# A hybrid decoder step on one core: issuing handed-over operations one step later, loading inner FFN tiles one by one, and pinning three groups of instructions

## The chip, the core and the metric

The kernel runs on one core of a Trainium2 chip. The core has a matrix engine (TensorE, PE in the profile, with a row of its own, PEld, for weight loads), a vector engine (VectorE, DVE), a scalar engine (ScalarE, ACT), a general engine (GpSimd, POOL) and an engine that here only issues transfers (SyncE, SP). Each engine takes its instructions from a queue of its own, in the order in which they stand there; 16 DMA engines move data between main memory and the on-chip memory. The metric is the device time of one execution in microseconds (us); less is better.

## The reference

One layer of a decoder trunk for 1024 prompt tokens and 64 sample tokens (8 sequences of 8 tokens), model width 1024, all in float32:

```python
x = x + 0.5 * swiglu(rmsnorm(x, norm_ffn1), ffn1_w_in, ffn1_w_out)     # inner width 2816
mix, new_pool, new_conv, new_ssm = token_mixing(rmsnorm(x, norm_mix), ...)
x = x + mix
x = x + 0.5 * swiglu(rmsnorm(x, norm_ffn2), ffn2_w_in, ffn2_w_out)
y = rmsnorm(x, norm_final)
```

`token_mixing` projects its input with `w_in`, and merges two branches with sigmoid gates. The pooling branch takes trailing-window means minus the token, multiplies them with a 256x256 matrix per group, scales them and applies `pool_w_out`. The SSD branch runs a causal convolution and a chunked state-space scan (32 heads of 64 in 4 groups, state 128, chunks of 128 tokens), gates its output with silu(z), normalises it in four groups and applies `ssd_w_out`. The merged branches go through `w_o`. The new pooling, convolution and state tensors are outputs as well.

## The kernel before

**Tokens and numbers.** The 1088 token columns are cut into two halves, h = 0 (512 prompt tokens) and h = 1 (512 prompt and 64 sample tokens). Activations lie with channels on the partitions. Every large product is made of three float32r matmuls: weights and activations are each split into a high part (ACT, a copy or identity) and a low part (DVE, source minus high part), and `products` issues high x high, high x low and low x high. `split` (L345 to L351) is that pair for activations, `load_w` (L277 to L296) loads a 256 KB block of weights and splits it. 90 blocks of later weights are split early by the generator `part_weights` (L298 to L311) while the first FFN runs, written to DRAM as two tiles and later read back ready-made (L287).

**Stages.** (1) Load and normalise x (`load_x`); first FFN, input side (`ffn_in_plain`, then `ffn_in`, a seven-product scheme) writing 22 inner tiles per half to DRAM (`hdram`); output side in `ffn`. (2) Input projection: `u_pair`, `z_pair`, `conv_pair`, `gate_pair`, with results written to DRAM. (3) The mix: pooling branch of half 0 and half 1 (`mix_pool`), then `ssd_out(0, 0)`, `mix_out(0)` (which calls `ssd_out(0, 1)` and applies `w_o`), `ssd_out(1, 0)`, `mix_out(1)`. Beside them runs the scan, a background job. (4) The second FFN and the final norm.

**What sets the order.** Background jobs are Python generators ("chains"). The code keeps a clock `pe[0]` that adds up the nominal time of each matmul that it issues; a chain that yields w is taken up again once the clock has moved on by w (`tick`, called after every few matmuls of the main work). The numbers at the head of the file (`STEP`, `GP`, `G_WAIT` and so on) are those yields. `until(c)` steps the chains without waiting for the clock until c has ended. The order in which the code issues instructions is a priority, not the final order: the compiler's scheduler may place an instruction ahead of earlier ones of its engine where it counts it as ready sooner. `tc.high_priority` moves an instruction's priority up.

**Buffers.** Most activation tiles come from one pool, `act`, of 58 buffers; FFN tiles also from `fx` (16), raw weights from `wraw` (6), split weights from `wh` and `wl` (3 each). An instruction that needs a buffer still in use waits at the head of its queue.

**The places that the change touches, before it:**

- Start (L802 to L814): x of half 0 is loaded in eight transfers, then four blocks of weights (`raws`), then x of half 1; the squares of x (L682) and the first `load_w` (L294) share ACT.
- `ffn`, L605 to L642: for each half, after the other half's or the input side's last matmul, all 22 inner tiles are loaded (L619, issued by POOL) and each is split at once (L620), then eight output columns m are accumulated over the 22 tiles.
- `pool_parts` (L1080): loads one tile `dd` of pooled inputs (L1084) and splits it at once (L1086). All eight of half 0 are asked for before the last `gate_pair`; of half 1, four while `mix_pool(0)` runs its last four `out(m)`, the rest inside the groups of `mix_pool(1)` (L1168 to L1170).
- The scan: for each half and group, `ssd_group` goes over 4 or 5 chunks with two steps each. `ssd_a` loads the decay rows `ab` (L1245, two buffers), transposes x (`pxT`), multiplies B and C (`pcb`), makes `cbm`, `btok`, `xp`, `xd` (L1255 to L1267), then `ea`, `ab` on ACT (L1272 to L1275) and the product `ab*cbm` on DVE (L1276). `ssd_st` multiplies `btok` and `xd` (`pst`) and updates the state `hst` (POOL L1361, DVE L1363); `ssd_b` makes the chunk's output (`pyo`, `pyd`, L1342 to L1344), and for the sample chunk handles eight state tiles `h0` (L1295 to L1329) with two loads in flight.
- `gating` (L1404): for each of four tiles a POOL product with z (L1412), at once its square on ACT and the running sum on DVE (`squares`, L364), then `rstd`, then the scaling (L1420) and the store to `yd`. Only two of the four z tiles are loaded ahead.
- `y_load` (L1431): loads eight `yd` tiles back (L1439), then splits one per step.
- `mix_out`, `merge(m)` (L1500): product with the gate, sum with the pooling branch on POOL (L1506), and its split at once.

```python
        def group(gi):                                            # mix_pool, L1167
            for k in range(2 * gi + 2, min(KD, 2 * gi + 6)):
                pool_parts(h, k, True)
            dh, dl = zip(pool_parts(h, 2 * gi), pool_parts(h, 2 * gi + 1))
```

Of the kernel before, what the change touches and what calls it, by code (L numbers as in the profile page):

```python
# [8 lines left out]
F32 = mybir.dt.float32  # L9
F32R = mybir.dt.float32r  # L10
# [33 lines left out]
STEP = (3.3, 3.3)  # L44
SSD0 = (2.0, 2.0)
C_PACE = 1.0
M_AT = (0.5, 1.0)
STEP_S = 1.8
GP = (0.7, 1.2)
# [10 lines left out]
N_PRE, N_DD = 3, 8  # L60
Y_PACE = 0.8
G_WAIT = (7.0, 5.0)
# [4 lines left out]
def tile_hybrid_pool_ssd_macaron(  # L67
# [203 lines left out]
    def raw_w(w, k0, nk, c0, ncol=P):  # L271
        raw = sp.tile([P, 4 * P], F32, tag="wraw", bufs=N_RAW, name=nm("wraw"))[:, : nk * ncol]
        dma(raw.rearrange("p (k c) -> p k c", c=ncol),
            w[k0 * P : (k0 + nk) * P, c0 : c0 + ncol].rearrange("(k p) c -> p k c", p=P))
        return raw

    def load_w(w, k0, nk, c0, ncol=P, raw=None):  # L277
# [15 lines left out]
        with tc.high_priority(hp[0]):  # L293
            S.activation(wh, raw, AF.Copy)  # L294
            V.tensor_tensor(wl, raw, wh.bitcast(F32), op=ALU.subtract)  # L295
# [302 lines left out]
    def ffn(wi, wo, prep, after, half=None, sums=None):  # L598
# [9 lines left out]
        for h in HALVES:  # L608
            for ff in range(NFF - N_APART, NFF):
                ffn_in(wi, ff, [(h, X[h])])  # L610
        for h in HALVES:
            N = NTOK[h]
            parts = [], []
            for k in range(NFF):

# [4 lines left out]
                split(t, a[:, :N], t.bitcast(F32R))  # L620
                parts[0].append(a)
                parts[1].append(t.bitcast(F32R))
            xt = []
            for ms in ((0, 1),) + tuple((m,) for m in range(2, KD)):
                po = [banks([(h,)], "pd", "po")[0] for _ in ms]
                for kb in range(0, NFF, 4):
# [150 lines left out]
    raws = [(kb, c0, raw_w(wi1, kb, 4, c0)) for kb in (0, 4) for c0 in (0, FF)]  # L777
# [4 lines left out]
    for kb, c0, raw in raws:  # L782
        ahead[kb, c0] = load_w(wi1, kb, 4, c0, raw=raw)
# [217 lines left out]
    def pool_out_rows(ost):  # L1001
# [5 lines left out]
        dma(new_pool_s[0, :, 0:7, :], state_pool[0, :, 8:HIST, :])  # L1007
# [72 lines left out]
    def pool_parts(h, k, only=False):  # L1080
        if (h, k) not in dparts:
            N = NTOK[h]
            dd = act((P, N), name="dd")
            dma(dd, ddd[k][:, slice(*TOK[h])])  # L1084
            a = act((P, N), F32R, "dh")
            split(dd, a, dd.bitcast(F32R))  # L1086
            dparts[h, k] = a, dd.bitcast(F32R)
        return None if only else dparts.pop((h, k))
# [40 lines left out]
    for k in range(N_DD):  # L1129
        pool_parts(0, k, True)  # L1130
    gate_pair(14, (1,))
    st.close()
# [29 lines left out]
    def mix_pool(h):  # L1162
# [42 lines left out]
    def sample_parts(g, Bf, xs4, dtd3):  # L1205


        out = []
        for i in range(2):
# [3 lines left out]
            S.copy(xr[:, 4, :].rearrange("p (r t) -> p r t", r=3), Bf[:, tok].unsqueeze(1).broadcast_to([P, 3, 32]))  # L1213
            px, pb = psum("ps", "px3"), psum("ps", "pb3")
            for j in range(4):
# [4 lines left out]
                            dtd3[:, i, g * HPG : (g + 1) * HPG].unsqueeze(2).broadcast_to([96, HPG, HD]), op=ALU.mult)  # L1220
            S.activation(X3, xd, AF.Copy)
            V.tensor_tensor(X3[32:64], xd[32:64], X3[32:64].bitcast(F32), op=ALU.subtract)
            B3 = small((96, P), "B3", 1, F32R)
            S.activation(B3, pb[:96, :P], AF.Copy)
# [3 lines left out]
                            bsel3.unsqueeze(2).broadcast_to([96, 4, P]), op=ALU.mult)  # L1228
            out.append((X3, bb))
        return out  # L1230

    def ssd_a(h, g, c, Bf, Cf, xs4, dts):
# [439 lines left out]
```

## Time and profile before

| what | us |
|---|---|
| median of 3 runs | 3068.37 (3059.94 to 3070.72) |
| the profiled execution | 3074.41 |
| its span, first to last instruction | 3072.5 |
| PE busy | 2888.5 (94%) |
| DVE, ACT, POOL busy | 1600.1, 1314.6, 854.2 |
| mean granted PE clock | 0.972 |

The profile page gives busy time by engine, 40 slices of the span, DMA queues, the chain that ended last and the costliest groups of instructions. The trace can be asked for waits (who waited for whom), for the instructions of a stretch in order of time, and for busy time in stretches of one's choice. "L165" is the line of the helper `mm` and "L169" that of `tr`, so matmuls and transposes are told apart by their tile names: `po` is the FFN's output, `pw` its input side and the projection, `pgm` and `pbp` the pooling branch, `pso` and `pwo` the products with `ssd_w_out` and `w_o`, and `pst`, `pyd`, `pyo`, `pxT`, `pcb` the scan.

### The profile page before, as it was taken

What the parts mean: (1) busy time and instruction counts of PE and PEld (TensorE: products, weight loads), DVE (VectorE), ACT (ScalarE), POOL (GpSimd) and SP (SyncE); (2) the same over time, 40 slices, a digit from 0 to 9 for tenths busy, and PEclk for the clock granted to TensorE, in tenths of its full rate; (3) what the DMA queues carried; (4) which work ended last, traced back from release to release, by engine and by line L of the source; (5) the groups of instructions that cost most, each with busy time, mean ns of one, the idle gap of its engine ahead of it and who ended that gap; (6) DMA issues with size and microseconds to landing.
All of it is one profiled execution on the core that took longest, in us unless ns stands there. A gap on an engine that the chain in (4) does not pass through costs nothing. (4 is left out here: it accounts for less than half of the span.)

```text
span 3072.5 us, 54064 instructions
## 1 busy us (share of the span) xinstructions
PE 2888.5 (94%) x20356; PEld 2721.6 (89%) x20356; DVE 1600.1 (52%) x2834; ACT 1314.6 (43%) x2755; POOL 854.2 (28%) x917
## 2 busy tenths in 40 slices
PE   6999999887999999999999799898899999999998
PEld 5999999667989999999987687777899999997898
DVE  5555445535355677666646565645355433344442
ACT  5344445423233346555556555434223333343332
POOL 4333333110043333333312222432114333332100
PEclk9999999998999999999999899997999999999999
DMA  4477667895353323233358687876775222226542
GB/s 125 145 242 235 204 204 230 287 293 171 105 193 113 106 89 123 87 105 106 108 195 281 226 301 254 277 236 217 252 262 174 88 78 82 71 84 206 167 134 73
DMA packets 531223, 532.33 MB, mean 173 GB/s; under 512 B 41530, under 2 KB 371376, under 8 KB 530954
## 3 DMA queue, kind: packets, MB, share of 16 engines
q1 hardware_dynamic: 523906, 504.37, 51.4%
q0 software_dynamic: 7040, 24.52, 2.2%
q8 instruction: 160, 2.62, 0.4%
q14 instruction: 101, 0.83, 0.1%
q10 hardware_dynamic: 16, 0.00, 0.0%
HBM read 377.09 MB, written 151.90 MB: 172 GB/s over the span
## 5 line engine op out<-in xcount | busy, mean ns | idle before, releaser
L165 PE MATMUL pw<-hi,wh 128*128 128x288 f32 (+1 forms) x2176 | 630.6, 290 | 8.4 <-DVE t L549 5.2
L165 PE MATMUL pw<-X,wh 128*128 128x256 f32 (+1 forms) x3264 | 627.9, 291 | 2.9 <-ACT rb L815 1.7
L165 PE MATMUL pw<-hi,wl 128*128 128x288 f32 (+1 forms) x2176 | 628.7, 289 | 0.7 <-DVE wl L445 0.7
L165 PE MATMUL pw<-lo,wh 128*128 128x288 f32 (+1 forms) x2176 | 628.3, 289 | 0.0
L165 PEld LDWEIGHTS pw<-X,wh 128*128 128x128 f32 x3264 | 519.9, 192 | 4.0 <-ACT rb L815 1.9
L165 PE MATMUL pw<-X,wl 128*128 128x256 f32 (+1 forms) x1632 | 473.3, 290 | 0.0
L165 PEld LDWEIGHTS pw<-hi,wh 128*128 128x128 f32 x2176 | 412.8, 190 | 9.6 <-DVE t L549 5.8
L165 PEld LDWEIGHTS pw<-hi,wl 128*128 128x128 f32 x2176 | 412.6, 190 | 0.9 <-DVE wl L445 0.9
L165 PEld LDWEIGHTS pw<-lo,wh 128*128 128x128 f32 x2176 | 412.7, 190 | 0.0
L445 DVE TENSOR_TENSOR wl<-s,wh 128x512 fp32r<-128x512 f32 x284 | 203.9, 720 | 256.1 <-ACT wh L444 251.9
L165 PEld LDWEIGHTS pw<-X,wl 128*128 128x128 f32 x1632 | 313.0, 192 | 0.2 <-DVE wl L445 0.2
L438 POOL TENSOR_TENSOR s<-wraw,wraw 128x512 f32<-128x512 f32 x142 | 195.2, 1375 | 416.8 <-DVE wl L445 295.1
L165 PE MATMUL po<-hh,wh 128*128 128x288 f32 (+1 forms) x1056 | 290.7, 334 | 17.3 <-ACT hh L347 12.9
L165 PE MATMUL po<-hh,wl 128*128 128x288 f32 (+1 forms) x1056 | 292.7, 332 | 5.1 <-DVE wl L295 4.8
L444 ACT ACTIVATE wh<-s 128x512 fp32r<-128x512 f32 x284 | 179.1, 631 | 269.8 <-PE pw L165 215.2
L165 PE MATMUL po<-hr,wh 128*128 128x288 f32 (+1 forms) x1056 | 293.1, 332 | 0.7 <-DVE hr L349 0.3
L295 DVE TENSOR_TENSOR wl<-wraw,wh 128x512 fp32r<-128x512 f32 x216 | 142.6, 665 | 262.3 <-ACT wh L294 258.2
L294 ACT ACTIVATE wh<-wraw 128x512 fp32r<-128x512 f32 x216 | 127.0, 596 | 305.5 <-PE po L165 249.4
L165 PEld LDWEIGHTS po<-hh,wh 128*128 128x128 f32 x1056 | 181.1, 192 | 36.7 <-ACT hh L347 16.5
L445 DVE TENSOR_TENSOR wl<-wraw,wh 128x512 fp32r<-128x512 f32 x213 | 157.4, 740 | 105.6 <-ACT wh L444 97.6
L444 ACT ACTIVATE wh<-wraw 128x512 fp32r<-128x512 f32 x213 | 134.1, 630 | 182.6 <-PE pw L165 163.3
L165 PEld LDWEIGHTS po<-hh,wl 128*128 128x128 f32 x1056 | 182.7, 192 | 21.9 <-DVE wl L295 7.8
(388 smaller groups left out, 5212.9 us busy)
## 6 DMA issues: line engine op xcount, KB each, us to landing
wraw<-in_ffn_w_in_dram SPq DMA_DIRECT2D x184, 256.0 KB
wraw<-wp SPq DMA_DIRECT2D x180, 256.0 KB
wraw<-in_ffn_w_out_dram SPq DMA_DIRECT2D x160, 256.0 KB
wraw<-in_w_in_dram SPq DMA_DIRECT2D x124, 256.0 KB
wp<-wp SPq DMA_DIRECT2D x90, 256.0 KB
wp<-wr SPq DMA_DIRECT2D x90, 256.0 KB
wh<-wp SPq DMA_DIRECT2D x90, 256.0 KB
wl<-wp SPq DMA_DIRECT2D x90, 256.0 KB
```

The lines of the kernel that those rows point to most:

```text
L165: T.matmul(out, lhsT, rhs, start=start, stop=stop, skip_group_check=free)
L294: S.activation(wh, raw, AF.Copy)
L295: V.tensor_tensor(wl, raw, wh.bitcast(F32), op=ALU.subtract)
L438: G.tensor_tensor(t, a, b, op=op)
L444: S.activation(wh, a, AF.Copy)
L445: V.tensor_tensor(wl, a, wh.bitcast(F32), op=ALU.subtract)
```

## The change

What is computed stays the same; issue order, yields and buffers change.

- **Start.** The four first weight loads and their ACT splits are pinned in program order (`keep_in_program_order` ties an instruction behind the one issued before it on its engine), so they stay behind x of half 0. The copy `new_pool_s <- state_pool` is pinned as well.
- **FFN inner tiles.** Loads become a chain `inner(h)`: one load per 0.4 (half 0) or 0.68 (half 1) of the clock, each split not before 3.5 after its load. Half 0's chain starts 2.0 into the last input column of half 1, half 1's with the last output column of half 0.
- **Pooled inputs.** `pool_parts` becomes `pool_load` and `pool_cut`. Half 0: eight loads, then eight splits at 0.8 each, all beside the last `gate_pair`. Half 1: two loads at each of `out(3)` to `out(6)` of half 0, and their splits one `out` later.
- **Scan.** `ab` is loaded after `ssd_b` of the chunk before; `ea` and `ab` come first in `ssd_a`, `xd` before `xp` and `cbm`; `ab*cbm` becomes `ssd_m`, a step later; the POOL product of the old state moves from `ssd_st` into `ssd_a`; `sample_parts` yields between its parts; three `h0` loads in flight instead of two, their POOL product right after the transposes. Steps: `STEP` 3.3 to 2.9, `SSD0` 2.0 to 3.0, `STEP_S` 1.8 to 1.6, one step fewer per group.
- **Gating.** All four z tiles are loaded ahead; four POOL products, after 6.5 four squares into four tiles, after 2.5 three sums; `G_WAIT` 7.0 to 4.0.
- **y_load and merge.** The DVE half of a split is issued one step after its ACT half; the split of `merge(m)` is issued with `merge(m + 1)`.

```diff
-    raws = [(kb, c0, raw_w(wi1, kb, 4, c0)) for kb in (0, 4) for c0 in (0, FF)]
+    raws = [(kb, c0, raw_w(wi1, kb, 4, c0, pin=True)) for kb in (0, 4) for c0 in (0, FF)]
...
-        ahead[kb, c0] = load_w(wi1, kb, 4, c0, raw=raw)
+        ahead[kb, c0] = load_w(wi1, kb, 4, c0, raw=raw, pin=True)
...
-        dma(new_pool_s[0, :, 0:7, :], state_pool[0, :, 8:HIST, :])
+        tc.keep_in_program_order(dma(new_pool_s[0, :, 0:7, :], state_pool[0, :, 8:HIST, :]))
...
             for k in range(NFF):
                 own = k < 3 if h == 0 else not half and k >= NFF - 2
...
                 G.dma_start(t, hdram[h][k])
-                split(t, a[:, :N], t.bitcast(F32R))
                 parts[0].append(a)
                 parts[1].append(t.bitcast(F32R))
+                todo.append((pe[0], t, a))
+                yield H_PACE[h]
+                while todo and todo[0][0] + H_LAND < pe[0]:
+                    cut()
+            while todo:
+                yield max(0.3, todo[0][0] + H_LAND - pe[0])
+                cut()
...
-            for k in range(2 * gi + 2, min(KD, 2 * gi + 6)):
-                pool_parts(h, k, True)
-            dh, dl = zip(pool_parts(h, 2 * gi), pool_parts(h, 2 * gi + 1))
+            dh, dl = zip(dparts.pop((h, 2 * gi)), dparts.pop((h, 2 * gi + 1)))
...
-            if h == 0 and m >= KD - 4:
-                pool_parts(1, m - KD + 4, True)
+            if h == 0 and m >= KD - 5:
+                for k in range(2 * (m - KD + 5), min(KD, 2 * (m - KD + 5) + 2)):
+                    pool_load(1, k)
+                if m > KD - 5:
+                    for k in range(2 * (m - KD + 4), 2 * (m - KD + 4) + 2):
+                        pool_cut(1, k)
...
         for c in range(n):
-            try:
-                next(ga)
-            except StopIteration as e:
-                a = e.value
-            if c + 1 < n:
-                ga = ssd_a(h, g, c + 1, Bf, Cf, xs4, dts)
-                next(ga)
+            a = yield from ssd_a(h, g, c, ab, Bf, Cf, xs4, dts)
             yield step
             if prev:
-                for w in ssd_b(h, g, *prev, Cf, y4, dts):
-                    yield w
+                yield from ssd_b(h, g, *prev, Cf, y4, dts)
+            if c + 1 < n:
+                ab = ssd_load(h, g, c + 1)
             yield step
+            ssd_m(a)
             prev = (c, a, ssd_st(h, g, c, a, dts))
...
         for j in range(4):
-            if j + 2 < 4:
-                z4.append(act((P, N), name="z"))
-                dma(z4[-1], zd[g * 4 + j + 2][:, slice(*TOK[h])])
             G.tensor_tensor(y4[:, j, :N], z4[j], y4[:, j, :N], op=ALU.mult)
-            squares(sums, y4[:, j, :N])
-            yield GP[0]
+        yield GP[0]
+        sq = [act((P, N), name="sq") for _ in range(4)]
+        for j in range(4):
+            S.activation(sq[j], y4[:, j, :N], AF.Square)
+        yield GP[2]
+        for j in range(1, 4):
+            V.tensor_tensor(sq[0], sq[0], sq[j], op=ALU.add)
```

More of the change, by code (lines that the diff above doesn't have):

```diff
@@ L607, in ffn, with inner, cut @@
             ffn_in(wi, ff, [(h, X[h]) for h in HALVES])
[L608 to L611, printed above, removed]
+        def inner(h):
             N = NTOK[h]
             parts = [], []
+            todo = []
+            def cut():
+                _, t, a = todo.pop(0)
+                split(t, a[:, :N], t.bitcast(F32R))
             for k in range(NFF):
@@ L619, in ffn @@
                 G.dma_start(t, hdram[h][k])
-                split(t, a[:, :N], t.bitcast(F32R))
                 parts[0].append(a)
                 parts[1].append(t.bitcast(F32R))
+                todo.append((pe[0], t, a))
[5 more added lines that the diff above has]
+                cut()
+            return parts
+        hid = {}
+        for h in HALVES:
+            for ff in range(NFF - N_APART, NFF):
+                ffn_in(wi, ff, [(h, X[h])])
+            if h == 0:
+                hid[0] = start(inner(0), H_AT)
+        for h in HALVES:
+            N = NTOK[h]
+            parts = None
             xt = []
@@ L625, in ffn @@
                 po = [banks([(h,)], "pd", "po")[0] for _ in ms]
+                if h == 0 and ms[-1] == KD - 1:
+                    hid[1] = start(inner(1), 1.0)
+                if parts is None:
+                    finish(hid[h])
+                    parts = hid[h].value
                 for kb in range(0, NFF, 4):
@@ L1078, in tile_hybrid_pool_ssd_macaron, with pool_load, pool_cut @@
     dparts = {}
[L1080 to L1088, printed above, removed]
+    def pool_load(h, k):
+        t = act((P, NTOK[h]), name="dd")
+        dma(t, ddd[k][:, slice(*TOK[h])])
+        dparts[h, k] = t
+    def pool_cut(h, k):
+        t = dparts[h, k]
+        a = act((P, NTOK[h]), F32R, "dh")
+        split(t, a, t.bitcast(F32R))
+        dparts[h, k] = a, t.bitcast(F32R)
     xn0 = []
@@ L1128, in tile_hybrid_pool_ssd_macaron, with first_pool @@
     gate_pair(14, (0,))
-    for k in range(N_DD):
-        pool_parts(0, k, True)
+    def first_pool():
+        for k in range(KD):
+            pool_load(0, k)
+            yield 0.3
+        for k in range(KD):
+            yield 0.8
+            pool_cut(0, k)
+    c = start(first_pool(), 0.5)
     gate_pair(14, (1,))
+    finish(c)
     st.close()
@@ L1346, in ssd_st @@
     def ssd_st(h, g, c, a, dts):
-        cd = dts[3]
-        btok, xd = a[4], a[2]
-        hc = c * NH + g * HPG
+        btok, xd, hn_ = a[4], a[2], a[8]
         hold = hstate[g]
@@ L1355, in ssd_st @@
         mm(pst, btok, xd)
-        hn_ = act((P, 512), name="hst")
         with tc.high_priority(HP_ST):
@@ L1442, in y_load @@
         yield 3.0
-        for a, t in zip(*parts):
-            split(t, a, t.bitcast(F32R))
+        for i in range(9):
+            if i < 8:
+                S.activation(parts[0][i], parts[1][i], AF.Copy)
+            if i:
+                a, t = parts[0][i - 1], parts[1][i - 1]
+                V.tensor_tensor(t.bitcast(F32R), t, a.bitcast(F32), op=ALU.subtract)
             yield Y_PACE
```

146 lines of the change are left out of this document (82 added, 64 removed).

## The prediction

> **What bounds the kernel now.** I read the page first, then busy time by stage, then PE's waits over the whole run.
>
> ```profile
> span 3072.5 us, 54064 instructions
> ```
>
> ```profile
> 0.00:500.00 500.00, 469.84 (x3551) 459.49 (x3552) 263.59 (x490) 231.46 (x517) 181.15 (x180) 0.99 0.61 193
> 500.00:900.00 400.00, 354.32 (x2062) 316.30 (x2060) 188.51 (x314) 143.61 (x268) 62.61 (x81) 0.95 0.68 218
> 1560.00:2200.00 640.00, 563.82 (x3603) 480.28 (x3602) 351.98 (x608) 315.28 (x710) 169.88 (x140) 0.93 0.77 255
> 2750.00:3073.00 323.00, 301.32 (x1872) 276.60 (x1870) 136.07 (x244) 109.49 (x209) 32.87 (x52) 0.97 0.46 143
> ```
>
> Columns: stretch, its length, busy us (instructions) of PE, PEld, DVE, ACT, POOL, then PE's granted clock, DMA share, GB/s. PE bounds every stage; what can be won is its idle time: 30.2 us around the start, 45.7 in the first FFN's output, 76.2 in the mix, 21.7 in the second FFN's output and the end, 174 in all. DVE and ACT are at 55% and 49% in the mix, so they are late, not full. Who was late:
>
> ```profile
> PE pst L165 <- DVE xd L1267: 20.1, 5, 8.5
> PE ptx L165 <- DVE dg L692: 19.2, 1, 19.2
> PE pss L165 <- DVE ssq L373: 16.8, 3, 14.3
> PE pgm L165 <- DVE fl L351: 14.6, 4, 8.9
> PE po L165 <- ACT hh L347: 12.9, 8, 5.2
> PE pso L165 <- ACT yh L347: 9.8, 2, 8.1
> PE pyd L165 <- DVE ab L1276: 8.6, 6, 2.7
> ```
>
> (us in total, times, longest.) These seven make 102 of the 174 us, and each is a place that the change touches. A long gap costs more than itself. The matmuls after the 5.2 us wait for `hh`:
>
> ```profile
> 553.83 0.63 PE L165 MATMUL po<-hr,wh 128*128 128x512 f32 x1
> ...
> 557.67 0.63 PE L165 MATMUL po<-hh,wl 128*128 128x512 f32 x1
> 558.10 0.63 PE L165 MATMUL po<-hh,wh 128*128 128x512 f32 x1
> ...
> 560.33 0.39 PE L165 MATMUL po<-hh,wl 128*128 128x512 f32 x1
> 560.56 0.39 PE L165 MATMUL po<-hh,wh 128*128 128x512 f32 x1
> ```
>
> They start 0.43 us apart until 558.10 and 0.23 apart later, so over some 5 us about 2.5 us are lost to the half clock. I add 2.5 us for each gap above 4 us. The Trainium skill (TensorE: Matmul & The Clock Gate, part 1) states that the clock halves after an idle window of about 3.4 us and returns after as long a busy one; by that each gap would cost 1.7 us, and the sum below would be about 5 us smaller. The trace agrees on the halving and shows the longer stretch.
>
> **1. Start: pinned weights.**
>
> ```profile
> 0.74 0.45 SPq L273 DMA_DIRECT2D wraw<-in_ffn_w_in_dram  x1
> ...
> 1.25 4.26 SPq L672 DMA_DIRECT2D xin<-in_x_prompt_dram  x8
> ...
> 12.40 0.63 ACT L294 ACTIVATE wh<-wraw 128x512 fp32r<-128x512 f32 x1 [7.09 <-DMA wraw<-in_ffn_w_in_dram]
> ...
> 18.10 0.61 ACT L682 ACTIVATE junk<-xin 128x512 f32<-128x512 f32 x1
> ...
> 21.70 5.32 PE L165 MATMUL ptx<-dg,xin 128*128 128x128 f32 x24 [19.18 <-DVE dg L692]
> ```
>
> The code issues x first, but a weight load stands ahead of it on SP, and on ACT the weight splits stand ahead of the squares and wait 7.09 us for their transfer. So the final order isn't the code's, and a pin has something to do. With the pin the squares follow x. The split at 12.40 had waited for the second block of weights, which is behind x, so x had landed by 12.4 at the latest. If the last two squares (0.61 each) end at about 12.4 to 13.5, and the rest of the chain keeps its 21.70 - 18.71 = 3.0 us, PE starts at 15.4 to 16.5: 5.2 to 6.3 us earlier. Against it, DVE may do the four low parts first, behind later weights. I take -5, bounds -2 and -7. The copy of the state, pinned too, leaves the start and lands where DMA has room; nothing for it.
>
> **2. FFN inner tiles.**
>
> ```profile
> 676.77 0.51 SPq L303 DMA_DIRECT2D wr<-in_ffn_w_in_dram  x1
> ```
>
> ```profile
> 693.89 0.63 ACT L347 ACTIVATE wp<-wr 128x512 fp32r<-128x512 f32 x1 [11.88 <-DMA wr<-in_ffn_w_in_dram]
> ```
>
> ```profile
> 680.00:700.00 20.00, 5.67 (x25) 4.40 (x24) 5.48 (x9) 6.62 (x12) 6.97 (x13) 0.72 1.05 391
> ```
>
> ```profile
> hr<-hd POOLq DMA_DIRECT2D x22, 288.0 KB, 6.7
> ```
>
> The 14.3 us wait of `pss` is this place: at the change of halves POOL's 22 loads fill the DMA engines (share 1.05), an early-weights block issued at 676.77 lands 17 us later, and ACT stands before it, with the last square of the norm and the splits of the new half behind. After the change the loads begin about a column earlier, but they still need buffers that the old half gives back tile by tile, and 22 x 288 KB in 22 x 0.68 us ask for 420 GB/s where 391 were moved. So part of the wait stays, at another place: I take half of 14.3 + 2.5, that is -8 (bounds +2 and -17). At half 0's start 5.2 + 2.5 are at stake; POOL's loads there no longer follow the gate product of the last column. I take -5 (bounds 0 and -8). The splits are issued 3.5 after a load that takes 6.7 to land (median), so ACT may wait at the head of its queue, with the weight splits and the copies that free PE's banks behind it. In the second FFN, where the change of halves shows no such wait, this could cost; I take 0 (bounds +5 and -5).
>
> **3. Pooled inputs of half 1.**
>
> ```profile
> ACT dh L347 <- DMA dd<-dd: 17.5, 7, 5.5
> ```
>
> ```profile
> 1705.50 0.61 PE L165 MATMUL pgm<-dh,wraw 128*128 128x288 f32 x1 [8.92 <-DVE fl L351]
> ...
> 1722.07 0.61 PE L165 MATMUL pgm<-dh,wh 128*128 128x288 f32 x1 [4.58 <-DVE fl L351]
> ```
>
> ACT, waiting in its queue for `dd`, holds back `fh`, hence `fl`, hence PE. With two loads per `out` (some 5 us of main work) and the splits one `out` later, all eight pairs are ready when half 1 begins. Gone: 8.92 + 4.58 + 2 x 2.5 = 18.5. On SP the eight loads move past the weights of four columns; next late there are the scan's own waits. I take -16 (bounds -8 and -18.5).
>
> **4. Gating and scan.**
>
> ```profile
> 1976.22 6.13 POOL L1412 TENSOR_TENSOR y<-z,y 128x576 f32<-128x576 f32 x4
> ```
>
> ```profile
> 1979.74 3.22 DVE L373 TENSOR_TENSOR ssq<-ssq,sq 128x576 f32<-128x576 f32 x2 [3.50 <-ACT sq L372]
> ...
> 1984.76 0.68 DVE L1267 TENSOR_TENSOR xd<-pxT,dts 128x512 f32<-128x512 f32 x1
> ```
>
> ```profile
> 1975.64 0.27 PE L169 MATMUL pcb<-ident,Bf 128*128 128x128 f32 x1
> ...
> 1985.58 2.05 PE L165 MATMUL pst<-xd,btok 128*128 128x512 f32 x2 [8.50 <-DVE xd L1267]
> ```
>
> The four products hand over one by one to ACT and DVE, which stand in between, and `xd` waits behind the sums. After the change the squares come 6.5 after the products (which take 6.13) and the sums 2.5 later, so neither engine stands; `xd` goes first, and `ab*cbm` is issued a step after ACT's part. At stake: 20.1 + 8.6 for `pst` and `pyd`, and about three gaps, 7.5, so 36. I take half, -18 (bounds 0 and -36), since the steps themselves get shorter.
>
> **5. The scan's end.** By the file's yields a group asks for 2.0 + 10 x 3.3 = 35.0 of the clock in half 0 and, with nine steps of 1.8, 2.0 + 12 x 3.3 + 16.2 = 57.8 in half 1; after, 3.0 + 9 x 2.9 = 29.1, and with fourteen steps of 1.6, 3.0 + 11 x 2.9 + 22.4 = 57.3. Eight groups: 371.2 to 345.6. Gating grows from 4 x 0.7 + 7 + 5 + 6.5 + 4 x 1.2 = 26.1 to 6.5 + 2.5 + 4 + 5 + 6.5 + 4.8 = 29.3. The last group is ready 22 us earlier.
>
> ```profile
> 2188.51 4.95 SPq L1439 DMA_DIRECT2D y<-yd  x8
> ```
>
> ```profile
> 2194.62 1.09 PE L165 MATMUL pso<-yh,wh 128*128 128x288 f32 x3 [8.14 <-ACT yh L347]
> ```
>
> The last `y_load` is issued as PE runs dry; 22 us earlier its load and splits hide beside `ssd_out(1, 0)`. 8.14 + 2.5: -10 (bounds 0 and -11).
>
> **6. What comes back.** More tiles are held (below), and chains are denser. The nearest row is one block of SP:
>
> ```profile
> SPq L287 <- PE pgm L165: 17.8, 3, 9.1
> ```
>
> I take one such block in PE, 9.1 + 2.5 = +12 (bounds 0 and +35 for three). Edits that I cost at nothing: `h0`'s third load, `merge`'s and `y_load`'s later halves, and half 0's pooled inputs, all hidden by main matmuls; without that cover a few us.
>
> **Sum.** -5 - 8 - 5 - 16 - 18 - 10 + 12 = -50 on the profiled execution's 3074.4 us (span 3072.5, 1.9 around it): 3024. It lay 6.0 above the median of the runs, so I forecast 3018.
>
> **Rivals.**
> *DMA stays the bound in the FFNs* (0.15). For it: share 1.05 in the row above, and the load's landing time of 6.7 against the 3.5 allowed. Then part 2 gives nothing and the second FFN loses 5: 3018 + 13 + 5 = 3036. The Trainium skill (DMA: Bandwidth & Descriptors, section on issuing engines) says the same as a rule: transfers from all issuing engines run on the same 16 DMA engines, so moving issue buys no bandwidth.
> *The scheduler's order, not the code's spacing, decides in the scan* (0.16). For it: before the 8.50 us wait that ended at 1985.58 PE ran out of work at 1977.08, barely 2 us after the transposes that `xd` reads, though the code puts two steps of 3.3 between `xd` and `pst`. Part 4 gives nothing: 3036. Against it: the handovers in ACT's and DVE's queues move as well.
> *No effect* (0.11): the scheduler restores nearly the old order: 3068.
> *Buffers run out, slower* (0.09). The change holds more of the 58 `act` buffers at once: eight more tiles of pooled inputs, two more z, two more squares, one more `h0`, copies of `B3`. A transfer whose buffer isn't free stands at the head of SP's queue with the weights behind. If each of eight groups meets a block like the 9.1 us one, 8 x 11.6 = 93 against the gains of 62: 3068 + 31 = 3099. It decides from 62 / 8 = 7.8 us per group on. Against it: the row counts three such waits in the mix now, not eight.
>
> **How the numbers follow.** The forecast case has 0.49. A measurement of this kernel tells about 0.5%, 15 us, from no change. Faster than 3053: the forecast, the first rival and nearly all of the second, 0.49 + 0.15 + 0.15 = 0.79; same: 0.11 + 0.01 = 0.12; slower 0.09. All gains in full and nothing back would be 7 + 30 + 18.5 + 36 + 11 = 102, some 2966; that everything works is unlikely, so the range begins at 2975. It ends at 3068, which holds both middle rivals and half of no effect; left out are the slower case, the other half and a small low tail, about 0.2.
>
> **What would show it.** Right: `ptx` starts at 15 to 17 us; no wait of `pgm` for `fl` above 2 us; `pst` and `pyd` together wait under 15 us; no 8 us gap before `ssd_out(1, 1)`; the mix's PE idle time falls from 76 to about 40 and its clock rises above 0.95. Wrong: SP waits of 9 us and more for buffers in the mix, `po` waiting for `wh` at the change of halves in the second FFN, or a mix as idle as before with other names in the list.

## The result and the profile after

| what | before | after |
|---|---|---|
| median of the runs, us | 3066.0 (3059.94 to 3070.72) | 3017.9 (3014.3 to 3018.36) |
| the profiled execution, us | 3074.41 | 3018.36 |
| its span, us | 3072.5 | 3016.4 |
| PE busy, us | 2888.5 | 2877.0 |
| PE idle (span less busy), us | 184.0 | 139.4 |
| mean granted PE clock | 0.972 | 0.980 |

The ratio of after to before is 0.984, with a 95% interval of 0.9815 to 0.9865. (One further run of after took 8222.61 us; it is in neither the range nor the ratio, and without it the median is 3017.44.) Of the 56.1 us of span, 44.6 are idle time of PE and 11.5 busy time: about the same number of matmuls took less time, and the mean granted clock rose from 0.972 to 0.980.

Where the stages begin, by the first matmul of a tile name (us from the span's start):

| stage | first tile | before | after | length before | length after |
|---|---|---|---|---|---|
| start | | 0 | 0 | 21.7 | 16.8 |
| first FFN, input side | `ptx` | 21.7 | 16.8 | 522.0 | 523.4 |
| first FFN, output side | `po` | 543.7 | 540.2 | 315.3 | 293.3 |
| projection | `pdt` | 859.0 | 833.5 | 736.0 | 730.6 |
| mix, to the last `pwo` | `pgm` | 1595.0 | 1564.1 | 705.9 | 679.1 |
| second FFN, input side | | 2300.9 | 2243.2 | 481.7 | 483.0 |
| second FFN, output side, and end | `po` | 2782.6 | 2726.2 | 289.9 | 290.2 |

So the change is worth 4.9 at the start, 22.0 in the first FFN's output side and 26.8 in the mix. The projection's 5.4 need care: with the FFN tiles alone, and with the pooled inputs alone (below), that stage took 730.6 and 730.4 us as well, and 732.8 with the scan alone. So 736.0 is the odd value, and the 5.4 are not put down to the change. The two stages that gave most, from busy time by stretch, first before, then after (columns as in the prediction):

```profile
543.70:859.00 315.30, 279.07 (x1594) 247.91 (x1594) 131.05 (x223) 103.58 (x182) 19.53 (x37) 0.94 0.65 210
1595.00:2300.90 705.90, 634.28 (x4121) 551.14 (x4121) 377.53 (x664) 315.07 (x702) 179.81 (x149) 0.93 0.78 259
```

```profile
540.20:833.50 293.30, 273.34 (x1593) 242.85 (x1594) 135.31 (x231) 106.90 (x189) 12.66 (x24) 0.97 0.68 216
1564.10:2243.20 679.10, 633.36 (x4120) 549.42 (x4121) 385.55 (x663) 313.86 (x702) 184.34 (x149) 0.95 0.82 269
```

The rows tell two different stories. In the FFN both idle time (36.2 to 20.0) and busy time (279.1 to 273.3) fell. In the mix idle time fell from 71.6 to 45.7, but busy time hardly moved (634.3 to 633.4), although fewer and shorter gaps should have left PE at the full clock for longer. Where that went is the main question below. PE's waits after, over the whole run (us in total, times, longest):

```profile
PE ptx L166 <- DVE dg L723: 14.3, 1, 14.3
PE po L166 <- ACT wh L297: 13.1, 8, 4.4
PE pss L166 <- DVE ssq L378: 10.4, 1, 10.4
...
PE pwo L166 <- DMA wraw<-wp: 7.3, 1, 7.3
PE prt L170 <- DVE rsm L367: 6.9, 4, 2.9
PE ph0T L170 <- DMA h<-in_state_ssm_dram: 5.9, 2, 5.4
...
PE pgm L166 <- DVE fl L356: 2.9, 1, 2.9
...
PE pst L166 <- DVE xd L1312: 2.5, 3, 1.1
```

Of the seven waits that the prediction listed, `pst` for `xd` (20.1) is down to 2.5, `pgm` for `fl` (14.6) to 2.9, and `pso` for `yh` and `po` for `hh` are gone. Three of 5 us and more are new: in the mix `pwo` for a weight block, 7.3, and `ph0T` for an old sample state, 5.4, and in the second FFN's input side one of `pw` for `t`, 5.6 (3.0 was the longest of that row before).

**The start.** From the order in time on ACT and DVE, then PE's start:

```profile
10.62 0.63 ACT L713 ACTIVATE junk<-xin 128x512 f32<-128x512 f32 x1
11.15 0.19 ACT L713 ACTIVATION_READ_ACCUMULATOR junk<-xin 128x1 f32 x1
11.52 0.63 ACT L297 ACTIVATE wh<-wraw 128x512 fp32r<-128x512 f32 x1 [0.18 <-DMA wraw<-in_ffn_w_in_dram]
```

```profile
12.18 0.69 DVE L300 TENSOR_TENSOR wl<-wraw,wh 128x512 fp32r<-128x512 f32 x1
13.09 0.69 DVE L300 TENSOR_TENSOR wl<-wraw,wh 128x512 fp32r<-128x512 f32 x1 [0.21 <-ACT wh L297]
13.99 0.69 DVE L300 TENSOR_TENSOR wl<-wraw,wh 128x512 fp32r<-128x512 f32 x1 [0.21 <-ACT wh L297]
...
16.44 0.87 DVE L723 TENSOR_SCALAR dg<-ident,xss 128x128 f32<-128x128 f32 x4
```

The squares of x now end at 11.3, ahead of the weights' splits. But DVE does three low parts between them and `dg`, 12.18 to 14.6, some 2.4 us.

**The change of halves.** On SP, then on ACT:

```profile
678.01 6.37 SPq L308 DMA_DIRECT2D wr<-in_ffn_w_in_dram  x1
```

```profile
691.74 0.63 ACT L352 ACTIVATE wp<-wr 128x512 fp32r<-128x512 f32 x1 [11.05 <-DMA wr<-in_ffn_w_in_dram]
693.73 0.63 ACT L377 ACTIVATE sq<-x 128x512 f32<-128x512 f32 x1 [0.84 <-DVE x L668]
```

The same early-weights block, issued at 678.01, still makes ACT stand, 11.05 us instead of 11.88, and the last square behind it still makes `pss` wait, 10.4 us.

**The new gap, and what follows it.** On SP (time, duration, issue), then on PE, then busy time by stretch:

```profile
1778.99 1.33 SPq L1489 DMA_DIRECT2D y<-yd  x3
1783.40 0.32 SPq L1221 DMA_DIRECT2D accd<-t  x1
1783.77 3.70 SPq L1489 DMA_DIRECT2D y<-yd  x5
1787.52 1.53 SPq L1356 DMA_DIRECT2D h<-in_state_ssm_dram  x3
```

```profile
1792.86 2.09 PE L170 MATMUL ph0T<-ident,h 128*128 128x128 f32 x8 [5.38 <-DMA h<-in_state_ssm_dram]
```

```profile
1792.80:1823.80 31.00, 30.95 (x127) 28.39 (x128) 10.02 (x15) 7.22 (x13) 8.58 (x8) 0.51 0.54 165
```

On SP, eight loads of `yd`, with a store between them that waited for its data, stand ahead of three loads of the old sample state. PE is out of work for 5.38 us. Then, for 31 us, PE is busy 30.95 us, at a granted clock of 0.51.

### The profile page after: what moved, and what is told of

Its sections match the earlier page's. It is cut to its first block, busy times and chain, and to the rows that moved or that the text cites. A ratio compares the mean times of both kernels' runs of the same rounds, so it can differ in the third digit from the quotient of the medians.

```text
span 3016.4 us, 54111 instructions
## 1 busy us (share of the span) xinstructions
PE 2877.0 (95%) x20356; PEld 2710.4 (90%) x20356; DVE 1608.8 (53%) x2834; ACT 1314.1 (44%) x2755; POOL 858.0 (28%) x917
## 4 chain that ended last, share of the span: by engine, by line
PE 75%; DMA 7%; issue 6%; DVE 4%; ACT 2%; POOL 2%; SPq 1%; ACTq 0%; DVEq 0%; POOLq 0%
PE pw L166 45%; PE po L166 10%; PE pso L166 6%; PE pwo L166 3%; PE pu L166 2%; PE pg L166 2%; DMA wr<-in_ffn_w_in_dram 1%; PE pbp L166 1%; PE pz L166 1%; DMA hr<-hd 1%; PE pyos L166 1%; DMA wraw<-wp 1%; PE pyd L166 1%; ACT ab L1301 1%; DMA wr<-in_w_o_dram 1%
## 5 line engine op out<-in xcount | busy, mean ns | idle before, releaser
L166 PEld LDWEIGHTS pw<-hi,wh 128*128 128x128 f32 x2176 | 412.8, 190 | 10.8 <-DVE t L554 10.2
L166 PEld LDWEIGHTS po<-hh,wh 128*128 128x128 f32 x1056 | 181.0, 190 | 30.6 <-ACT wh L297 17.5
L166 PEld LDWEIGHTS po<-hh,wl 128*128 128x128 f32 x1056 | 180.4, 189 | 26.9 <-DVE wl L300 13.3
```

Source lines behind the costliest of these rows:

```text
L166: T.matmul(out, lhsT, rhs, start=start, stop=stop, skip_group_check=free)
```

## The experiments

Twelve kernels were run, four at a time, each four on one chip with runs of the kernel before beside them; ratios are to those. One measure is used throughout: the length of a stage in the profiled execution. How far it wanders by itself shows in four builds whose code in the mix is that of after, untouched: 679.1 (after), 673.2, 673.0 and 667.5 us. A mix inside 667 to 679 is no different from after's. Each stage length comes from one execution, while the runs of one kernel spread by 4 to 24 us. After was run beside other runs of before (median 3066.0) than the twelve (3062.4 to 3066.79), so totals are compared with after's to some 5 us.

### The parts alone

**FFN tiles alone**: the kernel before with this part of the diff.

```diff
-                split(t, a[:, :N], t.bitcast(F32R))
...
+                todo.append((pe[0], t, a))
+                yield H_PACE[h]
+                while todo and todo[0][0] + H_LAND < pe[0]:
+                    cut()
```

> The kernel before with the chain for the inner FFN tiles alone. Own theory (each stage gains for itself): the first FFN's output side falls from 315 us to about 295, the second's stays at 290, the start and the mix stay as they were; 3044 to 3053 us in all. Rival (the DMA engines bound the change of halves, and the gain seen in that stage came from somewhere else, such as less traffic of the pinned state copy): the stage stays at 310 to 315 us, 3066 in all.

Measured: 3049.26 us, ratio 0.994 (0.9922 to 0.9958). The first FFN's output side took 293.1 us, start, second FFN's output side and mix were 21.4, 273.6 to the last `po` (273.0 before) and 710.8. The stage gains by this part alone; the rival falls. The mix, expected to stay, is 5 us longer than before's 705.9, and no run shows why.

```profile
543.60:836.70 293.10, 272.93 (x1594) 244.12 (x1595) 135.08 (x231) 106.44 (x189) 12.65 (x24) 0.97 0.68 217
```

**Pooled inputs alone.**

```diff
-            if h == 0 and m >= KD - 4:
-                pool_parts(1, m - KD + 4, True)
+            if h == 0 and m >= KD - 5:
+                for k in range(2 * (m - KD + 5), min(KD, 2 * (m - KD + 5) + 2)):
+                    pool_load(1, k)
+                if m > KD - 5:
+                    for k in range(2 * (m - KD + 4), 2 * (m - KD + 4) + 2):
+                        pool_cut(1, k)
```

> The kernel before with the pooled inputs' loads and splits moved, alone. Own theory: the waits of pgm for fl (14.6 us) go and the mix is some 16 us shorter, 3050 us in all. Rival (the scan's end sets the mix's end, so what the pooling branch gains is lost in a wait of the products with the scan's output): the pgm waits go, but waits of pso grow by as much, 3062 to 3066 in all.

Measured: 3047.57 us, ratio 0.9947 (0.9922 to 0.9973); mix 682.9 instead of 705.9. `pgm` still waits 4.4 us for `fl` in two places. `pso` waits 10.3 us for `yh` (9.8 before), so what was gained isn't lost there, and the rival falls. The wait at the scan's end is still there, as it should be:

```profile
2167.59 1.09 PE L165 MATMUL pso<-yh,wh 128*128 128x288 f32 x3 [8.37 <-ACT yh L347]
```

**Scan, gating, y_load and merge alone.** The rest of the mix's diff, with its steps:

```diff
-STEP = (3.3, 3.3)
-SSD0 = (2.0, 2.0)
+STEP = (2.9, 2.9)
+SSD0 = (3.0, 3.0)
...
-STEP_S = 1.8
-GP = (0.7, 1.2)
+STEP_S, N_H0 = 1.6, 3
+GP = (6.5, 1.2, 2.5)
...
+            ssd_m(a)
             prev = (c, a, ssd_st(h, g, c, a, dts))
```

> The kernel before with the scan, the gating, y_load and merge changed, with their new steps; start, FFN tiles and pooled inputs as before. Own theory (-18 -10 +12): 16 us less, 3050 us, the pst and pyd waits under 15 us in sum, and the 8 us wait of pso at ssd_out(1, 1) gone. Rival (the scan's gain needs the pooled inputs out of the way, the parts do not add): less than 5 us, 3061 to 3066.

Measured: 3033.39 us, ratio 0.9899 (0.9866 to 0.9932); mix 682.6. The own theory's sign holds and its size was too small. The profiled execution, 3044.74 us, is the slowest of this kernel's four, 11 us above their median, so its stage lengths may be too long. The waits of `pst` and `pyd` sum to 15.7 us by the four rows of them, a little over the 15 expected, and the wait of `pso` for `yh` is gone. Its two new gaps are here already: `pwo` for a weight block 7.8, `ph0T` for `h` 4.8.

The two parts of the mix alone gave 23.0 and 23.3, and together 26.8. The mix in busy time by stretch, pooled inputs alone and scan alone:

```profile
1590.60:2273.50 682.90, 619.40 (x4120) 536.26 (x4121) 375.06 (x663) 314.90 (x702) 180.32 (x149) 0.96 0.81 267
```

```profile
1593.70:2276.30 682.60, 630.91 (x4121) 548.43 (x4121) 387.38 (x665) 314.64 (x703) 186.66 (x149) 0.94 0.81 268
```

Split each into idle and busy time. Idle fell by 8.1 (71.6 to 63.5) and by 19.9 (to 51.7); both together, 25.9: idle time adds, nearly. Busy time fell by 14.9 (634.3 to 619.4) and by 3.4; both together, 0.9. What did not add is the clock, and most of it in the last part of the mix. From the first `pwo` to the last, in before, pooled inputs alone, scan alone and after:

```profile
1995.10:2300.90 305.80, 279.77 (x1881) 257.75 (x1879) 142.29 (x255) 97.23 (x209) 65.89 (x56) 0.91 0.74 242
1981.00:2273.50 292.50, 266.52 (x1880) 245.56 (x1879) 142.36 (x255) 97.27 (x209) 66.25 (x56) 0.96 0.77 253
2033.00:2276.30 243.30, 232.54 (x1624) 217.68 (x1622) 111.65 (x194) 61.55 (x125) 43.38 (x34) 0.97 0.79 265
1999.50:2243.20 243.70, 232.65 (x1623) 217.59 (x1623) 112.06 (x194) 61.96 (x127) 43.84 (x34) 0.97 0.80 266
```

The length times one minus the clock estimates the time lost to the half clock: 27.5 us, 11.7, 7.3 and 7.3. Each part alone takes away much of the same loss, 15.8 and 20.2 us, and both together take away 20.2. These 15.8 are most of the 17.4 us of busy time that are missing (14.9 + 3.4 - 0.9). The stretch at 0.51 above is little of it: with the scan alone, the 31 us from its first `ph0T` on ran at 0.63 already. For the pooled inputs, the 13.3 us gained in these rows lie where their code changes nothing. In their own place, from the first `pgm` to the first `pso`, they gained 11.9 (223.2 to 211.3).

By the medians of the runs the three parts alone gave 17.5, 19.2 and 33.4 us, 70 in all, and the whole change with its 4.9 at the start gave 48: the parts overlap in the totals as well.

### What in the scan

**Old pace**: after, with the scan's steps stretched so that it asks for as much of the clock as before.

```diff
-STEP = (2.9, 2.9)
+STEP = (3.2, 3.2)
...
-STEP_S, N_H0 = 1.6, 3
+STEP_S, N_H0 = 1.63, 3
```

> The kernel after with STEP 3.2 and STEP_S 1.63, so that eight groups ask for 4 x (3 + 9 x 3.2) + 4 x (3 + 11 x 3.2 + 14 x 1.63) = 371 of the clock, as before, and not 346. Own theory (the pace is worth the 10 us at the scan's end): the wait of pso before ssd_out(1, 1) is back with some 8 us, 3028 us. Rival (order and distance alone do it, the pace gives nothing): 3015 to 3021.

Measured: 3023.1 us (3014.55 to 3027.72), ratio 0.9864 (0.9832 to 0.9896); mix 678.1. `pso` does not wait for `yh` anywhere. The total lies between the two expectations, and its interval overlaps after's. What falls is the own theory's mechanism: the wait that the 10 us were worked out from is not back. From the order in time on SP, in this kernel:

```profile
2110.86 2.51 SPq L1474 DMA_DIRECT2D yd<-y  x4
```

and in before:

```profile
2179.28 2.51 SPq L1421 DMA_DIRECT2D yd<-y  x4
```

Counted from the first `pgm`, the last stores come at 584 before (2179.28 - 1595.0), at 549 with the old pace (2110.86 - 1562.3), and at 538 in after (2102.51 - 1564.1). Of the 46 us that the scan ends earlier, the pace made 10 and everything else 36 (the pooled inputs are part of that), and the 36 were enough.

**Old gating**: after, with the gating of before, its yields and its two z tiles loaded ahead.

```diff
         for j in range(4):
+            if j + 2 < 4:
+                z4.append(act((P, N), name="z"))
+                dma(z4[-1], zd[g * 4 + j + 2][:, slice(*TOK[h])])
             G.tensor_tensor(y4[:, j, :N], z4[j], y4[:, j, :N], op=ALU.mult)
-        yield GP[0]
...
+            squares(sums, y4[:, j, :N])
+            yield GP[0]
```

> The kernel after with the gating of before: two of four z tiles loaded ahead, each product followed at once by its square and running sum, and the old yields. Own theory (the handovers of gating in ACT's and DVE's queues held xd back): the waits of pst for xd come back with 8 us or more in the longest, the mix is 8 to 18 us longer than after's 679, 3026 to 3036 us. Rival (what helped is the new order in the scan alone, xd ahead of xp and cbm, and ab ahead of all): the mix within 4 us of after's.

Measured: 3012.31 us, ratio 0.9833 (0.9818 to 0.9848); mix 671.7, within what after's own code gives. In the waits of this kernel, the row that was 20.1 and 8.5 before:

```profile
PE pst L167 <- DVE xd L1313: 5.9, 4, 2.9
```

So the rival holds: with `xd` ahead in the scan's order, the gating's handovers no longer hold it back by 8 us, and the new gating shortens neither the mix nor the total in these runs. It isn't without effect: `pyd` waits 10.9 us for `ab` here, 2.6 in after, and the mix's idle time is 50.4 instead of 45.7. Busy time is 12.0 lower, mostly because the 31 us from the first `ph0T` on ran at the full clock (1.00) here. Against the build with the same busy time in the mix (667.5 us long, below), the old gating costs some 4 us, no more than such builds differ by themselves.

**No distance**: after's order, buffers and steps, with the operations at once behind what feeds them.

```diff
-GP = (6.5, 1.2, 2.5)
+GP = (0.7, 1.2, 0.7)
...
-G_WAIT = (4.0, 5.0)
+G_WAIT = (11.6, 5.0)
-H_AT, H_PACE, H_LAND = 2.0, (0.4, 0.68), 3.5
+H_AT, H_PACE, H_LAND = 2.0, (0.4, 0.68), 0.3
...
             a = yield from ssd_a(h, g, c, ab, Bf, Cf, xs4, dts)
+            ssd_m(a)
             yield step
...
-            ssd_m(a)
```

> The kernel after with its order, buffers and steps, but without the distance: squares and sums of the gating 0.7 instead of 6.5 and 2.5 behind what feeds them (the 7.6 saved are put into the wait behind the sums, so that the rest comes at the same clock), the product ab*cbm at once after the operations that feed it, and the inner tiles' splits 0.3 instead of 3.5 behind their loads. Own theory (the distance in the code removes the stalls): the waits of pst, pyd, pss and prt in the mix come back to 25 us or more, the mix is 10 to 18 us longer than after's 679, and the first FFN's output side 3 to 8 longer than 293; 3031 to 3044 us. Rival (the scheduler's order decides, whatever the code's spacing, and what helped is the order of operations inside a step and the loads that moved): within 5 us of the kernel after.

Measured: 3033.45 us, ratio 0.9895 (0.9855 to 0.9935); mix 687.6, first FFN's output side 299.7. The waits of `pst`, `pyd`, `pss` and `prt` in the mix sum to 31.1 us, 20.3 in after. New names among them:

```profile
PE pst L166 <- ACT ab L1301: 5.7, 1, 5.7
...
PE pst L166 <- ACT ea L1299: 3.5, 1, 3.5
```

The total is the own theory's; the mix grew by 8.5, a little less than its 10, and stands above all four builds with after's code there. Distance in the code does count, and not only order. Since the old gating costs so little, a likely carrier there is the product `ab*cbm`, which stands in DVE's queue until ACT has `ab` ready; that step was not tried by itself.

**Old states earlier**: after, with the first three loads of old sample states two steps earlier.

```diff
+            if c == 4:
+                pre = [h0_load(g, (i // 2, i % 2)) for i in range(N_H0)]
             yield step
             ssd_m(a)
...
```

> The kernel after with the first three loads of old sample states issued two steps (5.8 of the clock) earlier in each group of half 1. In the kernel after one of them lands 5.4 us late for PE at 1787.5, and from there PE runs 30.7 us at the half clock, though its idle time there is small. Own theory (the gap ahead of the light sample matmuls costs 5.4 plus about half of the 30.7): the gap and the long stretch go, the mix falls from 679 to 660 to 668, 3000 to 3008 us. Rival (the light matmuls, eight columns wide, hold the clock down themselves, gap or not): only the gap goes, the mix stays above 672. A second rival (three buffers held longer stop SP): slower than after.

Measured: 3000.23 us, ratio 0.9802 (0.9766 to 0.9838); mix 661.3. The gap is gone, and the 31 us from the first `ph0T` on ran at 0.89:

```profile
1787.50:1818.50 31.00, 26.00 (x177) 23.15 (x176) 14.89 (x25) 11.79 (x23) 13.41 (x12) 0.89 0.86 270
```

50 more matmuls fit into the same 31 us. That is the own theory's number. But the theory is only half shown. In the kernel of the next part, whose mix is after's, the gap stayed (4.85 us) and the stretch was short all the same:

```profile
1763.40:1794.40 31.00, 28.77 (x178) 25.32 (x179) 12.57 (x21) 12.83 (x26) 15.77 (x14) 0.84 0.77 233
```

And in the last kernel of this document, which has these loads early too, PE waits at most 1.4 us there, and the 31 us ran at 0.62:

```profile
1771.70:1802.70 31.00, 28.18 (x135) 26.18 (x134) 12.74 (x19) 8.88 (x16) 8.32 (x8) 0.62 0.63 205
```

So the gap is neither enough for a long stretch at the half clock nor needed for it, and the rival, that the light matmuls hold the clock down themselves, is not ruled out. What the edit is shown to save is idle time: the mix has 42.3 us of it here, 45.7 in after. Why the stretch was short here stays open.

### What is left at the change of halves

**Fewer early weights**: after, without the last four of the 90 blocks.

```diff
-    start(part_weights(early), W_AT)
+    start(part_weights(early[:-4]), W_AT)
```

> The kernel after without the last four of the 90 early weight blocks, the ones loaded from 660 us on (they are split later, in the second FFN). Own theory (ACT standing for wr at the change of halves makes the 10.4 us wait of pss): that wait falls to 5 us or less, the first FFN's output side from 293 to 284 to 288, 3008 to 3013 us. Rival (the DMA engines are full with the 22 tiles of half 1 and ACT would stand for those or for x from the spill instead): the wait stays at 8 to 11, under 3 us gained.

Measured: 3015.94 us, ratio 0.9845 (0.9812 to 0.9878). The wait of `pss` is gone and the output side took 286.4 us. So ACT's standing for these blocks is shown to be its cause. But the time did not fall with it: the four blocks, now split beside the second FFN, made its input side 493.7 instead of 483.0.

```profile
540.10:826.50 286.40, 273.22 (x1594) 243.17 (x1595) 132.96 (x227) 104.82 (x185) 12.72 (x24) 0.98 0.66 211
2229.70:2723.40 493.70, 480.12 (x3638) 471.95 (x3638) 217.45 (x377) 187.44 (x398) 173.72 (x168) 0.98 0.32 102
```

**Early weights one turn later**: the change's own idea, applied to `part_weights`. `put` loads a block; a block is loaded while the block before it waits for its split.

```diff
-        for w, k0, nk, c0, ncol in jobs:
-            t, a = fx(name="wr")[:, : nk * ncol], fx(F32R, name="wp")[:, : nk * ncol]
-            dma(t.rearrange("p (k c) -> p k c", c=ncol),
-                w[k0 * P : (k0 + nk) * P, c0 : c0 + ncol].rearrange("(k p) c -> p k c", p=P))
...
+        nxt = put(*jobs[0])
+        for i, (w, k0, nk, c0, ncol) in enumerate(jobs):
+            t, nxt = nxt, put(*jobs[i + 1]) if i + 1 < len(jobs) else None
             yield W_LAND
+            a = fx(F32R, name="wp")[:, : nk * ncol]
             split(t, a, t.bitcast(F32R))
             yield W_NEXT
```

> The kernel after with the early weight blocks handled as the change handles everything else: each block is loaded one turn of its chain before it is split, so that 6.5 and not 2.4 of the clock lie between load and split. Own theory (what is left of the wait at the change of halves is ACT standing at a split whose block has not landed): the pss wait of 10.4 us falls under 3, the first FFN's output side from 293 to 284 to 288 with the second FFN unchanged, 3008 to 3013 us. Rival (a third tile of the 16 in that pool makes loads wait for buffers and SP with them): the input side grows by as much or more, 3016 us and above.

Measured: 2979.09 us (2978.16 to 2987.77), ratio 0.9732 (0.9715 to 0.975): some 39 us below after by the medians, 33 by the ratios, far more than expected. Output side and mix:

```profile
535.80:804.90 269.10, 262.92 (x1594) 238.92 (x1594) 133.66 (x227) 105.00 (x184) 12.13 (x24) 1.00 0.73 234
1535.00:2202.40 667.40, 621.47 (x4120) 538.43 (x4121) 385.71 (x663) 313.12 (x702) 184.08 (x149) 0.97 0.83 274
```

24.2 us come from the output side, where PE is now idle for 6.2 us and its clock is 1.00; 4.0 from the input side (519.4); and 11.6 from the mix, where idle time is that of after (46.0 against 45.7) and busy time is 11.9 lower: mostly the shorter stretch at the half clock (31 us at 0.84 instead of 0.51, some 10 us). Why so much in the output side, ACT's waits from 500 to 760 show, in after:

```profile
ACT wp L352 <- DMA wr<-in_w_o_dram: 40.2, 13, 6.9
ACT wp L352 <- DMA wr<-in_ffn_w_in_dram: 35.4, 8, 11.0
```

ACT stood 75.6 us in 21 places for blocks that had not landed, with the splits of the FFN's own weights behind them in its queue. In this kernel no wait of ACT for `wr` is among the seven longest in that stretch, and `po` waits 3.4 us for `wh` there instead of 11.5.

**Both**, early weights one turn later and old states earlier (their two diffs together).

> The kernel after with the early weight blocks loaded one turn before their split and the first three old sample states loaded two steps earlier. If the two gains add (17 in the mix, 6 in the first FFN): 2992 to 2996 us. If a gain of one stage is lost in another: 2997 to 3003.

Measured: 2980.16 us (2972.99 to 2987.61), ratio 0.973 (0.9706 to 0.9753). Better than the expectation, but no better than the early weights alone: the mix took 668.4, without the gap, where it was 667.5 with it. The two gains do not add; what the earlier states seemed to win in after was mainly the one long stretch, and that was gone already. These two are the fastest kernels of the study, 27 per thousand below before and some 38 us below after (33 by the ratios).

### The low parts at the start

**Low parts behind `dg`**, alone (on after):

```diff
-        ahead[kb, c0] = load_w(wi1, kb, 4, c0, raw=raw, pin=True)
+        ahead[kb, c0] = load_w(wi1, kb, 4, c0, raw=raw, pin=True, lows=lows)
+    for _ in range(2):
+        prep1[0][0].step()
+    for wl, raw, wh in lows:
+        tc.keep_in_program_order(V.tensor_tensor(wl, raw, wh.bitcast(F32), op=ALU.subtract))
```

> The kernel after with the low parts of the four pinned weight blocks issued and pinned behind the diagonal blocks dg instead of ahead of them. In the kernel after DVE does three of them, 2.6 us, between the sums of squares and dg. Own theory: ptx starts at 14.0 to 14.6 us instead of 16.8, and all later stages shift by as much, 3015 to 3016 us. Rival: the low parts are late for the first pw or hold back hi and lo, and the input side grows by the 2 us that the start gained; 3018 us.

Measured: 3019.39 us, ratio 0.9854 (0.982 to 0.9888). `ptx` starts at 14.4, as the own theory has it, and then the input side grows by 8.9 us, to 532.3. The place is at its end:

```profile
537.67 0.63 ACT L355 ACTIVATE wp<-wr 128x512 fp32r<-128x512 f32 x1 [13.08 <-DMA wr<-in_ssd_w_out_dram]
```

**The same with early weights and old states earlier:**

> As the run before, with the low parts of the four pinned weight blocks behind dg as well. With them alone PE started 2.4 us earlier, but in that run ACT stood 13 us for an early weight block at the end of the input side. Own theory (that collision was met by chance of timing and not caused by the edit): with the blocks loaded earlier it is gone, and the 2.4 us stay, 2990 to 2994 us. Rival (the edit itself holds back the input side): no better than the run before, or worse.

Measured: 2988.45 us, ratio 0.9751 (0.9734 to 0.9768). The start took 13.7 us and the input side 521.1, 1.9 more than without it. But an early block met the inner tiles once more, at the change of halves:

```profile
676.15 0.63 ACT L361 ACTIVATE wp<-wr 128x512 fp32r<-128x512 f32 x1 [12.39 <-DMA wr<-in_ffn_w_in_dram]
```

and the output side took 287.1 instead of 271.9. So neither expectation holds as written: the edit itself hardly holds back the input side, and the collision came back at another place. The start's 2 us are real, but what they shift decides. Loading a block one turn ahead lessens this collision and does not exclude it.

## Why the prediction was right, and where it was not

The forecast of 3018 was met by 3017.9. The sign and the order of size are no accident, since each of the three places that were named gave its gain when it was tried. That the number fits to 0.1 us is luck: the profiled execution fell by 56 us where the sum had 50, 5.4 of it in the projection, and errors of single terms cancelled.

1. *Start, -5*: 4.9, and by the mechanism that was written. The low parts that were named as the thing against it took 2.4 us between x and `dg`.
2. *FFN tiles, -13*: 22.0 in the stage, and 22.2 with that part alone. The step that failed is the one for half 0's start, and the size of the one for the change of halves. At half 0's start `po` waited 5.2 for `hh`, and now waits 4.4 for `wh`: a wait took the place of the one removed. At the change of halves the wait of `pss` fell by only 3.9, since the block of early weights was still in ACT's way, as was argued. Most of the gain lay where no term stood: after that wait, in half 1, until the projection starts (before, then after).

```profile
698.60:859.00 160.40, 148.98 (x1065) 146.78 (x1066) 63.49 (x113) 46.47 (x80) 0.00 (x0) 0.96 0.39 124
695.10:833.50 138.40, 138.36 (x1023) 138.32 (x1024) 58.16 (x105) 42.77 (x72) 0.00 (x0) 0.98 0.44 137
```

   Of the 16.2 us of idle time that the stage lost, 11.4 lie here: `po` waited 4.8 for `wl` and 4.0 for `hh`. (The stretch is shorter by 22.0 also because some 40 of its matmuls now run ahead of that wait.) The second FFN, put at 0, gained nothing: 1.3 and 0.3 us longer.
3. *Pooled inputs, -16*: -23.0 alone, beyond the bound of -18.5, but only 11.9 of it in the place that the term is about: 8.8 of idle time and 3.1 of busy time, where 13.5 and 5 stood at stake. There the term was too large, though within its bounds. Most of the rest is the clock at the mix's end, which no term had and which the scan's part takes away as well.
4. *Gating and scan, -18*, and 5. *the scan's end, -10*: with what came back, -23.3 alone where -16 was forecast, and -33 by the medians. `pst` and `pyd`, 30.7 us before by their three rows (28.7 by the two in the prediction), wait 10.8 after by their four rows. But the reasons were wrong in two points. The gating is not what held `xd` back once `xd` stands first; the old gating costs some 4 us at most. And the scan's end did not need the shorter steps; the yields counted there made 10 us of 46.
6. *What comes back, +12*: the size and the engine were right, the reason was not. The two new gaps of PE in the mix are 5.4 and 7.3 us, both behind SP: before the first stand eight `yd` loads and a store, and before the second

```profile
2058.24 3.95 SPq L1489 DMA_DIRECT2D y<-yd  x8
2062.29 2.12 SPq L1389 DMA_DIRECT2D out_dram<-h  x3
2065.89 0.37 SPq L1449 DMA_DIRECT2D out_dram<-fin  x1
2066.36 2.57 SPq L290 DMA_DIRECT2D wraw<-wp  x1
```

the same loads of `yd` and stores of new states, ahead of a weight block. Neither was a buffer that ran out. What was missing is the half clock from the first of them on: 2.5 us were allowed, and the 31 us at 0.51 cost some 15 (31.0 x 0.49, an estimate that takes all of that work to run twice as fast at the full clock). That this is the price of the gap is not shown, since such a stretch also came without one.

So 3 to 6 together, forecast at -32, gave -26.8, and 2 made up for it. The parts alone would make a mix of 659.6 (705.9 - 23.0 - 23.3); builds with the same code there reached 667.5 at best.

Of the rivals, *DMA stays the bound in the FFNs* falls: with early weights one turn later the same inner tiles were moved, the DMA share rose to 0.73, and the stage took 269.1 us. It was a queue's head that waited, not the engines that were full all along; the Trainium skill's rule (DMA: Bandwidth & Descriptors, section on issuing engines), that all issuing engines share the same 16 DMA engines, is in keeping with the change of halves, where POOL's and SP's loads together filled them (share 1.04 from 680 to 700 us in after) and the early block landed late. It was no bound of the stage. *The scheduler's order, not the code's spacing* is nearly right for the gating and wrong for the rest, as far as the run without distance can show. *Buffers run out* and *no effect* did not come about: no wait of SP for a buffer in the mix exceeds 5.2 us.

Of the signs, `ptx` at 16.8, `pst` and `pyd` at 10.8, and no gap before `ssd_out(1, 1)` were as written. `pgm` has one wait of 2.9, where none above 2 was to be left. From 1560 to 2200 the mix's idle time is 46.2, not 40, and its clock 0.95, not above; that last sign was the one that pointed to the rest.

## What to carry to other kernels

Look at what an engine stands for at the head of its queue, not only at what PE waits for: a split issued before its block has landed holds up everything behind it, and loading one turn ahead was worth more for the early weights (28 of the 39 us lie in the first FFN) than for the inner tiles that the change was about. Test a part alone and then together, and compare idle time and busy time apart: idle time added up here, busy time did not, because two parts can take away the same loss of clock. When the start or a chain is shifted by a few us, look again at every later place where two chains can meet.

## What the runs showed of the hardware

PE at the half clock need not look idle. In after, PE was busy 30.95 of 31.0 us at a granted clock of 0.51, with the eight-column matmuls `pyos`, transposes and short runs of main matmuls between them; the `pso` matmuls that follow start 0.43 us apart until 1822.8, and 0.24 apart from there on. The Trainium skill (TensorE: Matmul & The Clock Gate, part 1) says that the clock returns after one busy window of about 3.4 us; the run agrees if such a stretch of light work does not count as busy, which no run here tests by itself. In seven builds that have after's mix, or that with the earlier old states, the 31 us from the first `ph0T` on had clocks of 0.51, 0.78, 0.83 and 0.84 behind gaps of 5.4, 4.9, 4.0 and 4.85 us, and 0.89, 0.88 and 0.62 without such a gap. What decides between 0.51 and 0.84 behind nearly the same gap, and between 0.62 and 0.89 without one, stays open. A free-running window, as the Trainium skill (TensorE: Matmul & The Clock Gate, part 1) states it, would allow this, and the runs cannot show it.
